# Seven-product units of the first projection, gate and up: the evacuation of a product is emitted ahead of the operands of a later one

## The chip, the cores and the metric

The kernel runs on one core of a Trainium2 chip. The metric is device time in microseconds (us); the time of a kernel is the median of several executions. Five engines matter: PE (matrix products; PEld is its weight load), ACT and DVE (elementwise work), POOL and SP (here they only issue transfers). Each engine runs its own instructions strictly in the order in which the program emits them, and waits on semaphores for what other engines or transfers have to finish first. So the place of a statement in the program is its place in the queue of its engine.

## The reference, cut to what matters

One encoder layer on 512 tokens of width 2048, in float32. The parts that the change touches are two groups of matrix products: part of the first projection, and gate and up of the feed-forward network.

```python
h = rmsnorm(x, attn_norm_w[l])
proj = h @ w_in[l]
...
aq, ak, av, gq, gk, gv, gr, glr = jnp.split(proj, split_idx, axis=-1)
...
mixed = jnp.concatenate([attn_out, gla_out], axis=-1) @ w_out[l]
x = x + mixed
h = rmsnorm(x, ffn_norm_w[l])
x = x + (jax.nn.silu(h @ w_gate[l]) * (h @ w_up[l])) @ w_down[l]
return rmsnorm(x, final_norm_w)
```

## The kernel before

**Precision.** A float32 operand is cut into a high part, rounded to the fast matrix format (`fp32r`), and a low part, the rest. A product is then high times high, high times low and low times high, added up in PSUM.

**Units.** Columns 256 at a time of a weight matrix make a unit. Its 2x2 block product is done by a scheme with seven products instead of eight (class `Units`, lines 1511 to 1654). The first projection (class `Front`, from line 1783) has 16 units: four of the output gate, four of the gated linear attention's q and k, eight of the attention's q and k. Gate and up (class `Feed`, from line 1656) have 44 units, gate and up in turn; the first two are done otherwise, and 42 go through the loop that the change touches.

**Steps.** A unit has seven steps, n = 0 to 6; step i of a stage is product n of unit u. Each product is 8 matmuls of 512 columns with the high part (line 1601) and 8 of 256 columns with the low part (line 1604). The products n = 0 to 6 go to the PSUM banks X, V, Y, X, W, Z, W, so several products add to a bank that an earlier one, or an evacuation, has filled.

**Operands** (`lead(i)`, called two steps ahead of product i): ACT casts the block to its high part (`cast`, line 1563), DVE adds two blocks for the product after that where n = 0, 1, 2 or 5 needs a sum (`add`, line 1538 and its neighbours: all four record as L1538), DVE subtracts the high part from the block to get the low part (`sub`, line 1569).

**Evacuation** (`evac_(i)`, called through `evac_late()` one step after product i was emitted). What it does depends on n:

- n = 0: ACT writes -X into bank Y (L1629)
- n = 1: ACT copies V to SBUF (L1632)
- n = 2: ACT writes -Y into bank W (L1636), DVE writes V - Y into bank Z (L1638)
- n = 3: ACT copies half of X (L1623), DVE adds the other half (L1624): one quarter of the unit's output tile, which is taken here
- n = 4: DVE adds W to the copy of V (L1645) and folds its halves into the output tile (L1647); product 6 adds to W and has to wait for L1645 to have read it
- n = 5, n = 6: a quarter of the output each (L1623, L1624); after n = 6 `finish` is queued for the next `run_urgent()`, which comes after the products of that step

`finish` scales the output tile on DVE (L1801 or L1799 in `Front`; L1727 for gate, L1734 for up) and POOL issues a store of it to DRAM, 512 KB (line 1802; line 1736 for up). Then the tile is given back.

**Tiles.** Blocks, sums, high parts, low parts and output tiles are all large tiles (`b` in the profile, 33 in the kernel). They are handed out first in, first out: `get` takes the tile that was given back longest ago, and the first instruction that writes it waits until the last user of the tile is done, be it PE, DVE or a store. `fetch()` (line 1524) is called at the head of each step: SP issues loads of weight blocks, 512 KB each, as long as fewer than 8 blocks are held and more than 3 tiles are free. A load waits on SP in the same way for the last user of its tile.

**The order of a step** is written out by hand in the two loops (lines 1766 and 1813): `fetch`, `lead` of the product two steps on, `evac_late` of the product before, then this step's products, then `run_urgent`.

Of the kernel before, what the change touches and what calls it, by code (L numbers as in the profile page):

```python
# [114 lines left out]
def put(*slots):  # L115
    for s in slots:
        if s.home is not None:
            s.home.free.append(s.i)


def layer(nc, tc, x, attn_norm_w, w_in, rel_table, gw_f, gb_f, gw_b, gb_b, gla_norm_w, w_out,
# [7 lines left out]
    with tc.manual_schedule(), \  # L129
# [136 lines left out]
        def run_urgent():  # L266
            while urgent:
                try:
                    next(urgent[0])
                    break  # L270
                except StopIteration:
                    urgent.popleft()
# [295 lines left out]
        def read_qk(pr):  # L568

            f = 1 - pr % 2  # L570
            if pr < NH // 2:
                mine = qkr[pr] = [[s2.get(F32R) for _ in range(2)] for _ in range(2)]
                for n in range(2):
                    for i in range(2):
                        src = qkd[pr // 2 * 2 + i][64 * n:64 * n + 64, f * 512:(f + 1) * 512]
                        for r in (slice(0, 64), slice(64, 128)):
                            pool.dma_start(out=mine[i][n].f[r], in_=src)
                            yield
# [168 lines left out]
        def attention():  # L747
# [7 lines left out]
            for u in range(UNITS + 5):  # L755
                h = u // 4
                if u < UNITS:
# [7 lines left out]
                    while h // 2 not in ready:  # L765
                        run_urgent()
                run(att_scores, u)
                run(att_round, u - 3)
                run(att_exp, u - 1)
                if u % 2 == 0:  # L770
                    run(att_lift, (u - 6) // 2, UNITS // 2)
# [65 lines left out]
        def gla_operands():  # L837
            G["raw"] = s2.get(F32, [P, KT, 32])
            sp.dma_start(out=G["raw"].t, in_=w_in[:, C_LR:C_LR + 32].rearrange("(k p) c -> p k c", p=P))
# [22 lines left out]
        def low_rank_weights():  # L862

            raw = G.pop("raw")
            w = G["w"] = [s2.get(F32R, [P, 8, 64]) for _ in range(2)]
            for i in range(2):
                r = raw.t[:, i * 8:(i + 1) * 8]
                act.copy(w[i].t[:, :, 0:32], r)
                dve.tensor_tensor(w[i].t[:, :, 32:64], r, w[i].f[:, :, 0:32], op=OP.subtract)
            put(raw)  # L870
# [785 lines left out]
        class Feed(Blocks, Units):  # L1656
# [82 lines left out]
            def run(self):  # L1739
                banks = {}  # L1740
                for i, (u, q) in enumerate(self.seq):
                    if u not in banks:
                        banks[u] = [ps.get() for _ in range(4)]
                    self.most = 5 if i < 2 else 3
                    self.load()
                    if i >= 5:
                        self.fetch((2, 3, 4)[i - 5])
                    self.split(i)
                    self.sums(i + 1)
                    self.sums(i + 2)  # L1750
                    self.split(i + 1)
                    if i < 2:
                        self.sums(self.n_sums, halves=True)
                    if i >= self.n - 2:
                        self.lead(i - self.n + 2)
                    self.pieces(i, banks[u])
                    done = None
                    if q == self.per - 1:
                        done = self.evac(u, banks.pop(u))
                        for _ in range((0, 2)[u]):  # L1760
                            next(done)
                    for _ in range(3 if i < 2 else 2):
                        run_urgent()
                    if done:
                        urgent.append(done)
                for i, (u, n) in enumerate(self.steps):
                    self.fetch()
                    self.lead(i + self.AHEAD)
                    self.evac_late()
                    self.products(i)  # L1770
                    if u == len(self.units) - 1:
                        if n in self.FREES:
                            for q in range(NP):
                                put(*xs[q]["slots"][self.FREES[n]])
                        if n in (1, 3, 5, 6):
                            down_start((1, 3, 5, 6).index(n))
                    for _ in range(2 if i < 7 else 1):
                        run_urgent()
                self.evac_late()
# [3 lines left out]
        class Front(Units):  # L1783
# [27 lines left out]
            def run(self):  # L1811
                assert len(xi) == NP
                for i, (u, n) in enumerate(self.steps):
                    self.fetch()
                    self.lead(i + self.AHEAD)
                    self.evac_late()
                    if u == len(self.units) - 1:
                        if n in (0, 2, 4):
                            st.until, st.limit = in_pieces, n // 2 + 1
                            st.load()  # L1820
                        if n == 6:
                            st.split(jobs[n_front].first + 2)
                    self.products(i)
                    if u == len(self.units) - 1:
                        if n in (4, 6):
                            for q in range(NP):
                                put(*xi[q]["slots"][self.FREES[n]])
                        if n == 4:
                            for _ in read_qk(0):
                                pass  # L1830
                        if n == 5:
                            gla_operands()
                    run_urgent()
                low_rank_weights()
                self.evac_late()
                run_urgent()
# [27 lines left out]
        def down_start(q):  # L1864
            if q == 0:
                g_load(0)
            if q == 1:
                st.until = down_pieces
                st.limit = 3
                st.load()  # L1870
                g_load(1)
            if q == 2:
                g_split(0)
                st.split(down_first + 2)
            if q == 3:
                dn.make(1)
# [497 lines left out]
```

## Time and profile before

| | us |
|---|---|
| time before, median of 3 runs (2161.77 to 2163.85) | 2162.83 |
| the profiled execution's own time | 2165.34 |
| its span in the trace | 2163.6 |
| PE busy | 2135.8 (99% of the span) |
| DVE busy | 1724.6 (80%) |
| ACT busy | 1229.1 (57%) |

Stages named here: `Front`, the units of the first projection, is in the stretch 105 to 450 us of the span; the loop of `Feed` is in 895 to 1720 us.

How to read the rows that follow. A row of the timeline has start and length in us, engine, line of the kernel, operation, output <- input by the program's names (a: small tiles, b: large tiles, ps: PSUM), shapes and count; in square brackets, how long the engine was idle before it, and what ended that. SPq and POOL rows with `DMA_DIRECT2D` are the issue of a transfer, not its run. A row of waits has total us, times, longest. A row of issues ends with the time from issue to landing. The row GB/s of a window gives the traffic in 40 equal slices of it. Busy PE is not PE at its peak, since matmuls are pipelined and their ends are modelled.

### The profile page before, as it was taken

How to read it: one execution, taken by the hardware profiler on the slowest of the kernel's cores; microseconds unless marked ns; L12 is line 12 of the kernel's file. 1: busy time of each engine (PE TensorE's matmuls, PEld its weight loads, DVE VectorE, ACT ScalarE, POOL GpSimd, SP SyncE). 2: the span in 40 equal slices, each digit the busy share in tenths (PEclk: the TensorE clock that was granted, in tenths of full speed). 3: DMA queues.
4: the chain of work that ended last, by engine and by line, in shares of the span. 5: the costliest groups of instructions: out<-in, count | busy, mean ns of one | idle time of the engine just before them, and what ended most of it. 6: DMA issues, size and time to landing. Idle time of an engine off the chain costs nothing.

```text
span 2163.6 us, 30507 instructions
## 1 busy us (share of the span) xinstructions
PE 2135.8 (99%) x11418; PEld 1835.3 (85%) x11418; DVE 1724.6 (80%) x2345; ACT 1229.1 (57%) x2051; POOL 172.6 (8%) x278
## 2 busy tenths in 40 slices
PE   9999999999999999999999999999999999999998
PEld 7887888888888888988888888888888888888887
DVE  5677787868877657988888888888888878897885
ACT  7444444457786545555545555555555576666762
POOL 0000000112312000000000000000000020232000
PEclk9999999999999999999999999999999999999999
DMA  6543444365754423444434334443344497899572
GB/s 203 172 149 108 136 120 134 105 199 171 201 199 140 134 98 117 137 127 123 116 113 136 116 118 117 127 132 112 114 130 117 173 241 248 200 256 241 194 256 78
DMA packets 340594, 330.47 MB, mean 153 GB/s; under 512 B 15133, under 2 KB 260365, under 8 KB 340446
## 3 DMA queue, kind: packets, MB, share of 16 engines
q1 hardware_dynamic: 313598, 258.07, 39.1%
q0 software_dynamic: 26528, 69.91, 12.5%
q8 instruction: 90, 1.47, 0.3%
q14 instruction: 58, 0.48, 0.1%
q10 hardware_dynamic: 320, 0.53, 0.1%
HBM read 267.55 MB, written 60.92 MB: 152 GB/s over the span
## 4 chain that ended last, share of the span: by engine, by line
PE 83%; issue 13%; DMA 1%; DVE 1%; ACT 1%; POOL 0%; DVEq 0%; SPq 0%; POOLq 0%; ACTq 0%
PE ps L1601 26%; PE ps L1604 14%; PE ps L349 6%; PE ps L350 6%; PE ps L348 6%; PE ps L2057 5%; PE ps L2056 5%; PE ps L2055 5%; PE ps L699 1%; PE ps L2270 1%; PE ps L2272 1%; PE ps L2271 1%; PE ps L643 1%; PE ps L724 1%; PE ps L723 1%
## 5 line engine op out<-in xcount | busy, mean ns | idle before, releaser
L1569 DVE TENSOR_TENSOR b<-b,b 128x1024 fp32r<-128x1024 f32 x406 | 495.2, 1220 | 133.9 <-ACT b L1563 122.0
L1563 ACT CAST b<-b 128x1024 fp32r<-128x1024 f32 x406 | 425.9, 1050 | 200.7 <-DVE b L1569 92.0
L1601 PE MATMUL ps<-a,b 128*128 128x512 f32 x1656 | 427.0, 393 | 16.4 <-DVE a L1645 11.1
L1601 PE MATMUL ps<-b,b 128*128 128x512 f32 x1592 | 421.2, 393 | 0.5 <-ACT ps L1629 0.5
L1601 PEld LDWEIGHTS ps<-a,b 128*128 128x128 f32 x1656 | 304.8, 189 | 81.9 <-issue 13.2
L1601 PEld LDWEIGHTS ps<-b,b 128*128 128x128 f32 x1592 | 280.2, 189 | 43.2 <-ACT ps L1629 0.7
L1538 DVE TENSOR_TENSOR b<-b,b 128x1024 f32<-128x1024 f32 x232 | 282.6, 1218 | 1.3 <-PE ps L350 0.7
L1604 PEld LDWEIGHTS ps<-b,b 128*128 128x128 f32 x1592 | 232.6, 190 | 23.4
L1604 PE MATMUL ps<-a,b 128*128 128x256 f32 x1656 | 242.9, 283 | 0.0
L1604 PE MATMUL ps<-b,b 128*128 128x256 f32 x1592 | 242.8, 282 | 0.0
L1604 PEld LDWEIGHTS ps<-a,b 128*128 128x128 f32 x1656 | 225.2, 192 | 8.5
L1623 ACT COPY b<-ps 128x256 f32<-128x256 f32 x174 | 64.6, 371 | 223.5 <-PE ps L1604 223.5
L2031 DVE TENSOR_TENSOR b<-b,b 128x1024 fp32r<-128x1024 f32 x112 | 136.5, 1220 | 34.8 <-ACT b L2023 34.8
L348 PE MATMUL ps<-b,b 128*128 128x512 f32 x344 | 139.8, 407 | 0.0
L350 PE MATMUL ps<-b,b 128*128 128x512 f32 x344 | 135.1, 393 | 0.0
L349 PE MATMUL ps<-b,b 128*128 128x512 f32 x344 | 134.9, 392 | 0.0
L2023 ACT CAST b<-b 128x1024 fp32r<-128x1024 f32 x112 | 116.6, 1052 | 26.6 <-DVE b L2011 15.3
L220 DVE TENSOR_TENSOR b<-b,b 128x512 fp32r<-128x512 f32 x120 | 79.5, 683 | 26.7 <-ACT b L239 26.5
L1624 DVE TENSOR_TENSOR b<-b,ps 128x256 f32<-128x256 f32 x174 | 72.2, 415 | 27.7 <-ACT b L1623 27.7
L2055 PE MATMUL ps<-b,a 128*128 128x512 f32 x240 | 93.4, 389 | 0.0
L2056 PE MATMUL ps<-b,a 128*128 128x512 f32 x240 | 93.4, 389 | 0.0
L2057 PE MATMUL ps<-b,a 128*128 128x512 f32 x240 | 93.4, 389 | 0.0
(308 smaller groups left out, 3580.6 us busy)
## 6 DMA issues: line engine op xcount, KB each, us to landing
b<-in_w_in_dram SPq DMA_DIRECT2D x94, 512.0 KB, 4.1
b<-in_w_gate_dram SPq DMA_DIRECT2D x88, 512.0 KB, 4.4
b<-in_w_up_dram SPq DMA_DIRECT2D x88, 512.0 KB, 3.8
b<-in_w_down_dram SPq DMA_DIRECT2D x88, 512.0 KB, 6.9
b<-in_w_out_dram SPq DMA_DIRECT2D x32, 512.0 KB, 4.4
md<-a POOLq DMA_DIRECT2D x56, 256.0 KB, 6.8
gd<-b POOLq DMA_DIRECT2D x22, 512.0 KB, 5.3
b<-gd SPq DMA_DIRECT2D x22, 512.0 KB, 5.5
```

The costliest lines, as they stand in the source:

```text
L348: mm(o, xh.t[:, c], wh.t[:, w], start=first and not on, stop=False, skip_group_check=on)
L349: mm(o, xh.t[:, c], wl.t[:, w], start=False, stop=False, skip_group_check=on)
L350: mm(o, xl.t[:, c], wh.t[:, w], start=False, stop=last, skip_group_check=on)
L1538: tt = lambda o, x_, y_: dve.tensor_tensor(o.t, x_.t, y_.t, op=OP.add)
L1563: act.copy(hi.t, home[key].t)
L1569: dve.tensor_tensor(lo.t, home[key].t, hi.f, op=OP.subtract)
L1601: mm(o.rearrange("p (s t) -> p s t", s=2), hi.t[:, q], self.xs[q][self.ORDER[n]], start=new and q == 0, stop=False, skip_group_check=True)
L1604: mm(o[:, 0:256], lo.t[:, q], self.xs[q][self.ORDER[n]][:, 0], start=False, stop=q == NP - 1, skip_group_check=True)
L2031: dve.tensor_tensor(lo.t, s.t, hi.f, op=OP.subtract)
L2055: mm(o, xh[:, t], wh, start=new and j == 0, stop=False, skip_group_check=True)
L2056: mm(o, xh[:, t], wl, start=False, stop=False, skip_group_check=True)
L2057: mm(o, xl[:, t], wh, start=False, stop=last and j == 1, skip_group_check=True)
```

## The change

In both loops `evac_late()` moves from behind `lead(i + AHEAD)` to ahead of it. Nothing is added or taken away.

```diff
                 for i, (u, n) in enumerate(self.steps):
                     self.fetch()
+                    self.evac_late()
                     self.lead(i + self.AHEAD)
-                    self.evac_late()
                     self.products(i)
                     if u == len(self.units) - 1:
                         if n in self.FREES:
...
                 for i, (u, n) in enumerate(self.steps):
                     self.fetch()
+                    self.evac_late()
                     self.lead(i + self.AHEAD)
-                    self.evac_late()
                     if u == len(self.units) - 1:
                         if n in (0, 2, 4):
                             st.until, st.limit = in_pieces, n // 2 + 1
```

On ACT the cast of product i + 2 now stands behind the evacuation of product i - 1, and on DVE the sum and the subtraction do. The output tile of a unit (taken by the evacuation of n = 3) is taken ahead of that step's high, sum and low tiles instead of behind them.

## The prediction

> **What bounds the kernel now.** I read first the windows of the two stages that the change touches, then who PE waited for in each (first two waits: 105 to 450 us; third: 895 to 1720 us).
>
> ```profile
> 105.00:450.00 345.00, 328.62 (x1839) 284.74 (x1838) 267.00 (x294) 157.77 (x219) 14.75 (x28) 1.00 0.46 133
> 895.00:1720.00 825.00, 824.54 (x4726) 725.55 (x4725) 700.72 (x760) 429.14 (x594) 11.17 (x21) 1.00 0.42 123
> ...
> PE ps L1601 <- DVE a L1645: 11.1, 12, 1.1
> PE ps L1601 <- ACT ps L1629: 3.5, 1, 3.5
> ...
> PE ps L1601 <- ACT ps L1629: 0.5, 1, 0.5
> ```
>
> `Feed` is bound by PE: 824.54 of 825 us busy, one wait of 0.5 us. There is nothing else to win there. In `Front` PE idles 16.4 us (345.00 - 328.62). Twelve units lose about 0.9 us each because product 6 waits for L1645, and 3.5 us go at the start. So I read one unit of `Front` in the timeline, from one scaling of an output tile to the next.
>
> ```profile
> 239.04 1.23 DVE L1801 TENSOR_TENSOR b<-b,a 128x1024 f32<-128x1024 f32 x1
> ...
> 240.56 0.53 POOL L1802 DMA_DIRECT2D gfd<-b  x1 [20.09 <-DVE b L1801]
> ...
> 243.53 1.05 ACT L1563 CAST b<-b 128x1024 fp32r<-128x1024 f32 x1 [3.33 <-DMA gfd<-b]
> ...
> 244.61 1.22 DVE L1569 TENSOR_TENSOR b<-b,b 128x1024 fp32r<-128x1024 f32 x1 [2.07 <-ACT b L1563]
> ...
> 246.95 1.23 DVE L1569 TENSOR_TENSOR b<-b,b 128x1024 fp32r<-128x1024 f32 x1 [1.12 <-ACT b L1563]
> ...
> 248.10 0.69 DVE L1638 TENSOR_TENSOR ps<-a,ps 128x512 f32<-128x512 f32 x1
> ...
> 248.69 1.22 DVE L1538 TENSOR_TENSOR b<-b,b 128x1024 f32<-128x1024 f32 x1
> ...
> 250.97 0.41 DVE L1624 TENSOR_TENSOR b<-b,ps 128x256 f32<-128x256 f32 x1
> ...
> 251.30 1.22 DVE L1538 TENSOR_TENSOR b<-b,b 128x1024 f32<-128x1024 f32 x1
> ...
> 253.57 0.68 DVE L1645 TENSOR_TENSOR a<-a,ps 128x512 f32<-128x512 f32 x1
> ...
> 254.39 2.08 PE L1601 MATMUL ps<-a,b 128*128 128x512 f32 x8 [0.85 <-DVE a L1645]
> ...
> 254.62 1.22 DVE L1538 TENSOR_TENSOR b<-b,b 128x1024 f32<-128x1024 f32 x1
> ...
> 255.76 1.22 DVE L1569 TENSOR_TENSOR b<-b,b 128x1024 fp32r<-128x1024 f32 x1
> ...
> 258.09 1.22 DVE L1569 TENSOR_TENSOR b<-b,b 128x1024 fp32r<-128x1024 f32 x1 [0.78 <-ACT b L1563]
> ...
> 259.23 0.41 DVE L1624 TENSOR_TENSOR b<-b,ps 128x256 f32<-128x256 f32 x1
> ...
> 259.68 1.22 DVE L1799 SCALAR_TENSOR_TENSOR b<-b,a 128x1024 f32<-128x1024 f32 x1
> ...
> 260.06 1.78 PE L1601 MATMUL ps<-a,b 128*128 128x512 f32 x7
> ...
> 262.85 2.00 PE L1601 MATMUL ps<-a,b 128*128 128x512 f32 x8
> ...
> 263.04 1.00 SPq L1531 DMA_DIRECT2D b<-in_w_in_dram  x2
> ```
>
> This is a **loop through a store**. The output tile is scaled (239.04) and stored (240.56). The cast of product 4 is handed that very tile and waits until the store has landed (243.53, idle 3.33 for the store). Subtraction 4, cast 5, subtraction 5 follow, and DVE works on without a pause until it waits for one cast (258.09) and scales the next tile (259.68). The loop takes 259.68 - 239.04 = 20.64 us. PE needs 2.79 us a product (262.85 - 260.06), 19.5 us a unit. PE waits out the difference at L1645.
>
> **The change part by part.** Per step ACT's evacuation moves ahead of one cast, DVE's ahead of at most one sum and one subtraction. Neither helper issues a transfer, so SP's and POOL's queues keep their order; PE's too, since only the evacuation holds matmuls there.
>
> *The loop, DVE's part.* Three terms change.
> - L1638 moves ahead of subtraction 5, into DVE's wait for cast 5 (idle 1.12 at 246.95): 248.69 - 248.10 = 0.59 off.
> - The last L1624 moves ahead of subtraction 2, into the 0.78 idle at 258.09: 259.68 - 259.23 = 0.45 off.
> - The L1624 of n = 5 loses that cover and stands ahead of a sum: 0.33 on (251.30 - 250.97).
>
> Those of n = 3 and n = 4 stay inside the loop. Sum: 20.64 - 0.59 - 0.45 + 0.33 = **19.93 us**, still over PE's 19.5.
>
> *The loop, the store's part.* L1645 gets ahead of a sum and a subtraction, while the scaling stays behind all of them. From L1645 to the scaling it is 6.11 us now (259.68 - 253.57). Then it is: 1.05 to the next sum (254.62 - 253.57), sum 1.14 (255.76 - 254.62), subtraction 1.14, L1624 0.33, sum 1.14, 2.33 between the last two subtractions (258.09 - 255.76), subtraction 1.14; together 8.27. PE runs on from L1645: product 2 of the next unit starts 262.85 - 253.57 = 9.28 behind it. That frees product 1's low tile, and SP issues two weight loads 0.19 later (263.04). The store is issued 1.52 behind the scaling (240.56 - 239.04). The first load follows the scaling by 3.36 now (263.04 - 259.68), and by 9.28 + 0.19 - 8.27 = 1.20 then. So **the load goes from 1.84 us behind the store to 0.32 ahead of it.** The second load needs a tile that a sum frees, 1.14 + 1.14 + 1.22 = 3.5 behind the scaling.
>
> What such a meeting costs shows in `Feed`: its up units issue the same store (landing us: `Front`'s median in the first row, min, median, max of `Feed`'s 22 in the second), a load 0.27 ahead of it (939.82, 940.09).
>
> ```profile
> gfd<-b POOLq DMA_DIRECT2D x4, 512.0 KB, 2.9
> ...
> DMA to landing us min/median/max: 2.9/5.3/6.3
> ...
> 939.82 6.74 SPq L1531 DMA_DIRECT2D b<-in_w_gate_dram  x3
> 940.09 0.54 POOL L1736 DMA_DIRECT2D gd<-b  x1 [35.26 <-DVE b L1734]
> ...
> GB/s 0 0 0 0 0 0 0 0 0 0 0 20 59 193 225 219 207 197 242 217 361 408 432 432 426 328 180 49 0 0 0 0 0 0 43 113 152 272 319 342
> ```
>
> The last row is the traffic from 938 to 948 us, 0.25 us a slice: about 2.5 us at some 220 GB/s, then 1.5 at 430. The store seems to wait out the load. In `Feed` nobody needs its tile at once; in `Front` a cast does. Call d what the landing takes beyond 2.9. Bounds: 0 (no meeting; less than 0 is excluded, since 2.9 is `Feed`'s minimum too) and 6.3 - 2.9 = 3.4. I take the nearest row, the median: **d = 5.3 - 2.9 = 2.4**, and a loop of 19.93 + 2.4 = 22.33 us, 1.7 more than now. Nothing corrects it: scaling and load both hang on L1645. Of the second load I count nothing; it is what the upper bound is for.
>
> *Start and end.* Here the trace reads:
>
> ```profile
> 114.18 1.04 ACT L1563 CAST b<-b 128x1024 fp32r<-128x1024 f32 x1 [2.42 <-DMA vd<-b]
> 115.13 0.58 ACT L1629 ACTIVATE ps<-ps 128x512 f32<-128x512 f32 x1
> ...
> 117.54 1.22 DVE L1569 TENSOR_TENSOR b<-b,b 128x1024 fp32r<-128x1024 f32 x1
> ...
> 133.38 1.22 DVE L1801 TENSOR_TENSOR b<-b,a 128x1024 f32<-128x1024 f32 x1
> ...
> 383.80 1.23 DVE L1801 TENSOR_TENSOR b<-b,a 128x1024 f32<-128x1024 f32 x1
> ...
> 399.89 2.06 PE L1601 MATMUL ps<-a,b 128*128 128x512 f32 x8 [1.06 <-DVE a L1645]
> ```
>
> The 3.5 us wait goes: L1629 no longer queues behind the cast at 114.18. PE doesn't keep it, because DVE is next: from subtraction 4 (117.54), DVE's chain needs the loop without its store, 19.93 - (244.61 - 239.04) = 14.36, so the first scaling comes at 131.90 (now 133.38). The last stalled product is that of 399.89, product 6 of the fourteenth unit; its scaling before is that of 383.80, the thirteenth, twelve loops behind the first. Afterwards no blocks are left to load, tiles are plenty, and PE sets the pace. From a scaling to that product it takes 19.93 - 8.27 + (254.39 - 253.57) = 12.48, plus d. After: 131.90 + 12 x 22.33 + 12.48 + 2.4 = 414.74, that is 14.85 later than 399.89. In general the change is 13 d - 16.35, and it breaks even near d = 1.3.
>
> *Feed.* Its loop hides the store (no wait on it), so the order costs DVE cover only. DVE works 700.72 us in 42 units, 16.7 of 19.6 each; the tightest result, L1645, comes ahead of a sum and a subtraction instead of behind them. I count no loss. The start's 0.5 goes, since L1629 no longer stands behind a cast. If the cover is gone after all, each 0.1 us a unit costs 42 x 0.1 = 4.2.
>
> *Sum.* +14.85 - 0.5 = +14.4 us. The profiled execution took 2165.34, 2.5 above the median of the runs; on it 2179.7, on the median 2162.83 + 14.4 = **2177.2 us**.
>
> **A rule weighed.** The traffic row says that the store waits while the load runs. The Trainium skill, "DMA: Bandwidth & Descriptors", section "Queues, rings and completion order", says that each DMA engine takes turns between its queues, packet by packet. By that the two would share; the row's 220 followed by 430 GB/s speaks for the waiting, so I keep the row's price. What sharing would give is the second rival.
>
> **The rivals.**
> 1. *The store stays clear of the load* (d near 0), so the shorter loop pays. For it: `Front`'s stores land in 2.9 today, and my 0.32 is a difference of chains of seven terms; half a microsecond of DVE less would turn the order round. Against it: at equal issue the two still meet. Time: -16.35 - 0.5 = -16.8; with the strays of today's loop, (383.80 - 133.38) - 12 x 20.64 = 2.7 and (399.89 - 383.80) - (254.39 - 239.04) = 0.7, it is -13.4: **2149.4**. This is the other side: one mechanism, the landing, decides at d = 1.3.
> 2. *Store and load take turns.* The store alone bursts 1.4 us (524 KB at the 430 GB/s of the late slices is 1.2); turns would at most double that: d = 1.4, 13 x 1.4 - 16.8 = +1.4, **2164.2**. Against it: the median of 5.3.
> 3. *The second load is waited out too.* d = 3.4, 13 x 3.4 - 16.8 = +27.4, **2190.2**. For it: the load is issued 2 us behind the store, while the store is still waiting. Against it: by then the store's packets are queued.
>
> That the order doesn't change is no case: the program fixes it.
>
> **How the numbers follow.** Forecast (d about 2 to 3) 0.50, rival 3 and beyond 0.17, rival 2 0.11, rival 1 0.22. A measurement here tells 0.2% (4.3 us) from no change: slower means d above 1.6, faster d below 1.0. So slower 0.67, same 0.11, faster 0.22. Cases of both signs hold the range: from rival 1, 2149, to just past rival 3, 2191. The forecast's own range, d from 2 to 3, is 2172 to 2185.
>
> **What would show it.** Right: in `Front` the store's landing near 5.3, the cast's wait for it longer than 3.33, scalings 22.3 apart, PE waiting for the cast or L1636 at product 4 and for L1645 at product 6, no 3.5 us at the start; `Feed` as before, with its 0.5 gone. Wrong: scalings 19.9 apart with landings of 2.9 (rival 1), near 21.3 (2) or beyond 23 (3); any PE wait that recurs in `Feed`; or a tile that a cast is handed with another last user than today, which would break the loop I summed.

## The result, and the profile after

| | median us | runs |
|---|---|---|
| before | 2162.3 | 2160.89 to 2163.85, 4 |
| after | 2176.94 | 2171.53 to 2178.09, 4 |

The ratio is 1.0063, with a 95% interval of 1.0044 to 1.0082: slower by 14.6 us, where 2177.2 us was forecast. The profiled execution took 2178.09 us (forecast 2179.7), its span is 2176.3.

The windows of the two stages (`Front`, then the loop of `Feed`) in the changed kernel:

```profile
105.00:450.00 345.00, 318.65 (x1759) 276.65 (x1758) 256.90 (x280) 153.38 (x206) 13.48 (x26) 0.98 0.43 119
...
905.00:1735.00 830.00, 830.00 (x4765) 730.88 (x4765) 710.12 (x769) 427.25 (x599) 11.17 (x21) 1.00 0.42 124
```

`Feed` now has no gap at all. `Front`'s stretch holds 80 matmuls fewer than before (1759 against 1839): there the time went. Who PE waited for in it:

```profile
PE ps L1601 <- ACT ps L1636: 21.8, 10, 3.5
PE ps L1601 <- DVE a L1645: 4.5, 9, 0.6
```

Before, L1645 had 11.1 us and the start 3.5. That part of the change worked: the start's wait is gone, and L1645 comes earlier. A new wait takes their place, product 4 for L1636, which on ACT stands behind the cast that waits for the store. One unit in the timeline of the changed kernel, from scaling to scaling:

```profile
242.53 1.22 DVE L1801 TENSOR_TENSOR b<-b,a 128x1024 f32<-128x1024 f32 x1
...
243.72 2.74 SPq L1531 DMA_DIRECT2D b<-in_w_in_dram  x2
...
244.04 0.53 POOL L1802 DMA_DIRECT2D gfd<-b  x1 [23.57 <-DVE b L1801]
...
249.76 1.04 ACT L1563 CAST b<-b 128x1024 fp32r<-128x1024 f32 x1 [5.45 <-DMA gfd<-b]
...
250.71 0.58 ACT L1636 ACTIVATE ps<-ps 128x512 f32<-128x512 f32 x1
...
250.84 1.22 DVE L1569 TENSOR_TENSOR b<-b,b 128x1024 fp32r<-128x1024 f32 x1 [4.82 <-ACT b L1563]
...
251.34 1.88 PE L1601 MATMUL ps<-a,b 128*128 128x512 f32 x7 [2.08 <-ACT ps L1636]
...
251.98 0.69 DVE L1638 TENSOR_TENSOR ps<-a,ps 128x512 f32<-128x512 f32 x1
...
253.18 1.23 DVE L1569 TENSOR_TENSOR b<-b,b 128x1024 fp32r<-128x1024 f32 x1 [0.51 <-ACT b L1563]
...
256.92 0.68 DVE L1645 TENSOR_TENSOR a<-a,ps 128x512 f32<-128x512 f32 x1
...
257.75 2.06 PE L1601 MATMUL ps<-a,b 128*128 128x512 f32 x8 [0.55 <-DVE a L1645]
...
265.19 1.22 DVE L1799 SCALAR_TENSOR_TENSOR b<-b,a 128x1024 f32<-128x1024 f32 x1
```

Read it from the top. The load is issued at 243.72, the store at 244.04: 0.32 us ahead, to the hundredth as summed. The cast waits 5.45 us for the store (3.33 before), L1636 follows it at 250.71, and PE has stood for 2.08 us. L1638 now lies in DVE's wait for cast 5. From L1645 to the next scaling it is 8.27 us (265.19 - 256.92), the sum of the prediction. The whole loop takes 22.66.

Whose packets moved is in the rows of the two queues (packets, MB, share), first from 245 to 247 us, then from 247 to 249; q1 carries the loads, q0 the store:

```profile
q1 hardware_dynamic: 615, 0.31, 80.7%
...
q0 software_dynamic: 139, 0.52, 63.5%
q1 hardware_dynamic: 536, 0.27, 44.4%
```

The store was issued at 244.04; alone, its bytes move from 1.0 to 2.4 us after the issue. Here, with the loads on the way, q0 has not a single packet up to 247, 3 us after the issue, and then all its 0.52 MB go in 2 us. The same two rows for the 4 us behind the issue, 244.04 to 248.04, say how much went first:

```profile
q1 hardware_dynamic: 1040, 0.52, 58.9%
q0 software_dynamic: 57, 0.23, 14.2%
```

The 1040 packets and 0.52 MB of q1 are one load, the one ahead; the second load, issued behind the store, is not yet among them. The store waits until the load ahead of it has gone; the two do not take turns. Whether it is held in its queue or on the way from POOL's issue into the queue, no row here shows.

### The profile page after: what moved, and what is told of

The parts are those of the page before. It is cut to its first block, busy times and chain, and to the rows that moved or that the text cites. A ratio compares the mean times of both kernels' runs of the same rounds, so it can differ in the third digit from the quotient of the medians.

```text
span 2176.3 us, 30564 instructions
## 1 busy us (share of the span) xinstructions
PE 2139.1 (98%) x11418; PEld 1837.9 (84%) x11418; DVE 1727.0 (79%) x2345; ACT 1226.5 (56%) x2051; POOL 172.5 (8%) x278
## 3 DMA queue, kind: packets, MB, share of 16 engines
q0 software_dynamic: 26528, 69.91, 12.5%
## 4 chain that ended last, share of the span: by engine, by line
PE 83%; issue 13%; DMA 1%; DVE 1%; POOL 0%; ACT 0%; SPq 0%; DVEq 0%; POOLq 0%; ACTq 0%
PE ps L1601 26%; PE ps L1604 14%; PE ps L350 6%; PE ps L349 6%; PE ps L348 6%; PE ps L2057 5%; PE ps L2055 5%; PE ps L2056 4%; PE ps L699 1%; PE ps L643 1%; PE ps L723 1%; PE ps L724 1%; PE ps L2272 1%; PE ps L2270 1%; PE ps L2271 1%
```

## The experiments

The quoted texts say what was expected of each run before it was made.

**e1 and e2: each loop alone.** The edit of the change in `Front` alone, then in `Feed` alone.

> The new order in Front alone, the old one in Feed. My theory (the whole loss is Front's loop through the store): 2162.3 + 14.9 = 2177 us, units of Front 22.5 us apart, stores landing in about 5.5 us; only Feed's 0.5 us wait at its start comes back. Rival A (the order costs DVE cover in Feed's 42 units, and that is what was lost): near 2162 or below, with Front's shorter DVE chain even 2149. Rival B (half and half): about 2170.

> The new order in Feed alone. My theory: 2161.8 us, the 0.5 us wait at Feed's start gone and nothing else; no PE wait in Feed. Rival A: up to 15 us slower, 2177. Rival B: about 2169.

Measured: `Front` alone 2177.66 us against 2162.31, ratio 1.0071 (1.0056 to 1.0086). `Feed` alone 2162.09, ratio 0.9996 (0.9987 to 1.0006). All of the loss is `Front`'s; in `Feed` the order makes no difference that can be measured. Rivals A and B fall.

**e3 and e4: the loads held until the store has landed.**

```diff
                     self.evac_late()
                     self.lead(i + self.AHEAD)
+                    if n == 2:
+                        sp.dma_start(out=held[u], in_=self.both[i + 2][0].f[0:1, 0])
```

e3 does this in the new order, e4 in the old one. The small transfer reads the high tile of product 4, so SP stands there until the cast that waits for the store is done; the loads are queued behind it.

> Both loops in the new order, and in each unit of Front SP issues a 512-byte transfer out of the high tile of product 4 before the next two weight loads, so that these cannot be issued before the cast that waits for the store is done. Order of ACT and DVE and the tiles handed out are those of the change. My theory (the store waits for the load that is ahead of it): stores land in 2.9 us, units 19.9 us apart, 13 x 0 - 16.8 us on 2162.3: 2145.5. Rival (the casts are late because evacuations stand ahead of them, and the landing is only what is seen of it): units still 22 us apart, about 2177. Rival (turns: the store loses 1.4 us to any load): about 2164.

> The old order with the same held loads: the control for e3. My theory: each unit 20.64 us, the strays of landings over 2.9 us (3.5 us in all) gone: 2159. If holding the loads costs something by itself (a load that comes too late, a busy SP): above 2162.3, and e3 has to be read against it. If the loads had no part in the strays: 2162.

Measured: e3 2148.96 us, ratio 0.9937 (0.992 to 0.9953): 13.3 us faster than the kernel before, 28 faster than the change. One unit of e3 in the timeline:

```profile
251.87 1.22 DVE L1801 SCALAR_TENSOR_TENSOR b<-b,a 128x1024 f32<-128x1024 f32 x1
...
253.38 0.53 POOL L1804 DMA_DIRECT2D gfd<-b  x1 [19.40 <-DVE b L1801]
...
256.35 1.05 ACT L1563 CAST b<-b 128x1024 fp32r<-128x1024 f32 x1 [2.69 <-DMA gfd<-b]
...
257.43 0.25 SPq L1820 DMA_DIRECT2D held<-b  x1
...
257.78 10.00 SPq L1531 DMA_DIRECT2D b<-in_w_in_dram  x4
...
271.80 1.22 DVE L1803 TENSOR_TENSOR b<-b,a 128x1024 f32<-128x1024 f32 x1
```

The loads come behind the cast, and the loop takes 271.80 - 251.87 = 19.93 us, the prediction's sum with nothing added for a later landing. ACT and DVE run in the order of the change; only the meeting of load and store is gone. So it is the meeting that costs, and the order by itself gains. The run is 3.5 us above the 2145.5 expected; two late landings, 4.1 and 4.0 us instead of 2.9, are 2.3 of that.

e4, the control, is 2163.2 us, ratio 1.0003 (0.9994 to 1.0012). Holding the loads costs nothing that can be measured, but my 2159 was a miss: the late landings of the old order are still there, with the loads far away. For the one issued at 195.05 us in e4, the queues and the landing in the 4 us behind the issue:

```profile
q0 software_dynamic: 142, 0.52, 33.5%
q8 instruction: 1, 0.02, 1.5%
...
grd<-b POOLq DMA_DIRECT2D x1, 512.0 KB, 4.7
```

A packet of the instruction queue q8 is there. In e3 and e4 each store of `Front` that landed later than 3.2 us had one in the 4 us behind its issue (e3: 4.1 and 4.0; e4: 4.7 and 3.5), and no other one of the loop's stores had one of q8. That is a coincidence, not an experiment, and e5 and e6 weaken it: seven of their stores had such a packet, and four of these landed in 2.9 to 3.2.

**e5 and e6: the store's tile out of the loop.** `Front` holds at most 6 blocks instead of 8, so its queue of free tiles is two longer, and the tile of the store goes to a weight load.

```diff
+            def fetch(self, most=6):
+                Units.fetch(self, most)
+
             def place(self, u):
                 return self.units[u]
```

> The old order; Front holds at most 6 blocks instead of 8, so two more tiles are free and the tile of the store is handed to a weight load (which nobody waits for soon) instead of to the cast of product 4. My theory (the loop through the store bounds Front): no loop, PE sets the pace after the 3.5 us wait at the start, product 6 of the fourteenth unit at about 383.3 us instead of 399.9: 2162.3 - 16.6 = 2145.7 us. Rival (DVE is too busy for PE's pace, whatever tile a cast gets): units stay near 20.6 us, 2160 to 2163. Rival (6 blocks are too few, loads come late): slower, with casts waiting for loads.

> The new order with at most 6 blocks. My theory: the same, and without the 3.5 us wait at the start and its slow clock: product 6 of the fourteenth unit at about 378.5 us: 2162.3 - 21.4 - 0.5 = 2140.4 us; landings may still be 5 us, without a wait for them. Rival (the loss comes from the order of casts behind evacuations): slower than e5 by the 14.6 us of the change, about 2160.

Measured: the old order (e5) 2142.37 us, ratio 0.9907 (0.9892 to 0.9922); the new order (e6) **2140.81 us**, ratio 0.9898 (0.9884 to 0.9913). Both beat both kernels. `Front`'s window in e5:

```profile
105.00:450.00 345.00, 344.70 (x1945) 299.60 (x1944) 282.33 (x325) 170.91 (x247) 20.89 (x40) 1.00 0.51 147
```

PE is busy for 344.70 of 345 us, and scalings are 19.55 us apart. What waits for the 14 stores issued up to 400 us in e5 is now SP with its loads, up to 12.5 us each. DVE was never too slow for PE: in either order the loop through the store was what kept `Front` behind PE's pace. e5 came 3.3 us below its 2145.7, because the 3.5 us wait at the start, which I had left in, is not in it either. Without the loop the change costs nothing: the old order keeps a 0.5 us wait at the start of `Feed`, which the new one has not; the medians are 1.6 apart, each compared with the kernel before rather than with each other.

**e7: at most 7 blocks, new order.** The edit of e6 with 7.

> The new order with at most 7 blocks: one more free tile, so the store's tile goes to the low tile of product 4 (the subtraction waits for the store, not the cast: 1.08 us less in the loop), the cast of product 5 no longer waits for subtraction 4 (1.2 us less), and both loads of the step are issued ahead of the store. My theory (the store waits out every load issued ahead of it, 2.4 us each): landing 2.9 + 4.8 = 7.7 us, loop 19.93 - 2.28 + 4.8 = 22.5 us, about as slow as the change, 2177. If it waits out one load only: landing 5.3, loop 20.1 us, about 2148.

Measured: 2166.4 us, ratio 1.0018 (1.0009 to 1.0028), between the two values. The timeline of one unit of e7, and then the row of the landing of its store (us from issue):

```profile
260.21 0.53 POOL L1805 DMA_DIRECT2D gfd<-b  x1 [21.65 <-DVE b L1802]
...
267.09 1.23 DVE L1569 TENSOR_TENSOR b<-b,b 128x1024 fp32r<-128x1024 f32 x1 [4.90 <-DMA gfd<-b]
...
268.23 0.69 DVE L1638 TENSOR_TENSOR ps<-a,ps 128x512 f32<-128x512 f32 x1
...
268.83 1.22 DVE L1569 TENSOR_TENSOR b<-b,b 128x1024 fp32r<-128x1024 f32 x1
```

```profile
gfd<-b POOLq DMA_DIRECT2D x1, 512.0 KB, 6.8
```

The subtraction waits for the store, as said. Two loads ahead, issued 1.25 and 0.29 us before this store, make the landing 6.8, 3.9 more than alone: neither one load's 2.4 nor twice that. In the 4 us behind its issue q1 moved 1846 packets and the store 6, so part of the second load went ahead of it too. (The thirteen stores of the loop land in 5.0 to 7.2.) And L1638 is back in the loop (268.83 - 268.23 = 0.60), since cast 5 no longer makes DVE wait. With that the loop should be 19.93 - 2.28 + 0.6 + 3.9 = 22.15; from the scaling at 258.70 to that at 280.83 it is 22.13.

**e8: only the second of the two loads held, new order.**

```diff
+                    if n == 3:
+                        self.fetch(min(8, len(self.quads) + 1))
+                        sp.dma_start(out=held[u], in_=self.both[i + 1][0].f[0:1, 0])
                     self.fetch()
```

> The new order; of the two weight loads of step 3 in Front the first is issued as in the changed kernel, the second held (as in e3) until the cast that waits for the store is done. My theory (the first load, 0.32 us ahead of the store, is what it waits out; the second costs nothing): landings 5.3 to 5.5 us, units 22.3 us apart, 2175 to 2177 us, as the change. Rival (the second load, issued 2 us behind the store, is what delays it): landings near 2.9 to 4, 2149 to 2163. If both have a share: between, near 2170.

Measured: 2173.72 us, ratio 1.0049 (1.0032 to 1.0066), a little under the forecast. SP in the timeline of one unit of e8 and the landing of its store (issued at 264.17):

```profile
263.84 0.37 SPq L1531 DMA_DIRECT2D b<-in_w_in_dram  x1
...
270.79 0.25 SPq L1818 DMA_DIRECT2D held<-b  x1
...
271.13 0.37 SPq L1531 DMA_DIRECT2D b<-in_w_in_dram  x1
```

```profile
gfd<-b POOLq DMA_DIRECT2D x1, 512.0 KB, 5.5
```

With the second load out of the way the store still lands at 5.5. The first load, 0.33 us ahead, is what it waits out. In five of e8's loops the load came 0.4 us behind the store instead, and those stores landed in 3.6 to 3.7 us; that fits a time a little under the forecast.

## Why the prediction was right

*The bound.* `Front` was held by the loop through the store, and `Feed` by PE: shown by e1, e2 and by e5, where one number takes the tile out of the loop and PE waits 0.2 us in all.

*The loop's DVE part, 19.93 us.* Shown by e3, to the hundredth.

*The order of load and store.* 0.32 us ahead, as summed. That the meeting is what costs is shown by e3 against the change: 28 us apart with the same order on ACT and DVE.

*The landing.* Summed with 5.3; most stores of the changed kernel land in 5.4 to 5.7. The store waits the load out; the turns by packet that the Trainium skill states ("DMA: Bandwidth & Descriptors", "Queues, rings and completion order") are not seen in the rows of the queues here: one whole load, 1040 packets, went first.

*The new wait.* Product 4 for L1636 and product 6 for L1645, as named.

*The sum.* The fourteenth unit's product 6 was summed to 414.74 and started at 413.96. Four sizes behind that were off, and they nearly offset each other:

- The first scaling came at 129.78, not 131.90. The stage before had been 2.1 us faster in that execution, and it is no part of the change: e4, in the old order, shows 1.9 of it. Counted from the first product of `Front` (106.31 before, 104.19 after) the first scaling came 1.48 us sooner, as summed.
- "Nothing corrects it" was wrong. In three of the twelve loops the store landed in 3.9 us, and the loop took 20.9. The rows below are from the changed kernel: PE clock by windows, then the timeline.

```profile
160.00:164.00 4.00, 3.08 (x11) 2.57 (x12) 3.08 (x4) 2.19 (x4) 0.00 (x0) 0.77 0.03 8
164.00:168.00 4.00, 4.00 (x22) 3.60 (x21) 3.96 (x6) 2.11 (x2) 0.00 (x0) 0.80 0.34 86
```

```profile
160.92 2.29 PE L1601 MATMUL ps<-a,b 128*128 128x512 f32 x7 [1.93 <-ACT ps L1636]
...
165.15 2.23 PE L1601 MATMUL ps<-b,b 128*128 128x512 f32 x8
...
176.28 0.53 POOL L1802 DMA_DIRECT2D grd<-b  x1 [22.00 <-DVE b L1801]
...
176.74 0.37 SPq L1531 DMA_DIRECT2D b<-in_w_in_dram  x1
```

  Behind a wait the granted clock fell to 0.77, and product 4 took 165.15 - 160.92 = 4.23 us instead of 2.79. That used up PE's wait for L1645 and more: product 6 of that unit started 15.92 us behind the scaling, instead of 15.22 in the unit shown above. So the next load, which follows PE, was issued at 176.74, 0.46 behind the store instead of 0.32 ahead. The store kept its place, and the next unit came sooner. The same pair, a slow product 4 and then a landing of 3.9, recurs from 273.85 and from 362.48.
- The other nine loops took more than 22.33: 22.5 to 22.7, and one 24.1. That one's store landed in 7.1 us, with a packet of the instruction queue behind its issue.
- From the thirteenth scaling to the fourteenth unit's product 6 it took 413.96 - 397.27 = 16.69 us, against the 14.88 summed. The store in it landed in 6.3 us instead of 5.3, and behind the wait of 2.71 us that followed, the granted clock fell to 0.58 (408 to 412 us).

The mean of the twelve loops is (397.27 - 129.78) / 12 = 22.29 us, against the 22.33 of the prediction. Counted from the first product, the whole stretch grew by 16.2 us, against the 14.85 summed. That the forecast of 2177.2 fits the median of 2176.94 this closely is in part luck: the four runs alone lie between 2171.53 and 2178.09. The sign and the mechanism are not luck.

*The rivals.* The one on the other side, a store clear of the load, was priced at 2149.4; e3 makes it true and takes 2148.96. Turns, priced at 2164.2, would have made landings of 2.9 + 1.4 = 4.3 us; most are 5.4 to 5.7. The wait for the second load, priced at 2190.2, is excluded by e8.

## What to carry to other kernels

Where a tile goes straight from a store to the next user, the landing is part of a loop, and its length hangs on which transfers are issued just ahead; look up from both sides what an edit does to that order, even if it moves no transfer. Here the new order shortened DVE's part of the loop by 0.71 us and lost more than that, because the load, which follows PE, moved 2.16 us forward against the store. The cheaper cure here was one number, the depth of the prefetch: two free tiles more took the store out of the loop and were worth more than either order.

## What the runs showed of the hardware

- A 512 KB store issued 0.3 us behind a 512 KB load moved no packet for 3 us and mostly landed in 5.4 to 5.7 us instead of 2.9; issued 0.4 to 0.5 us ahead of it, in 3.6 to 3.9; with two loads ahead, in 5.0 to 7.2. The transfer that came first moved its data first, though the two come from different queues.
- A packet of the instruction queue behind a store's issue went with a later landing: 4.8 and 3.6 us in the kernel before, 4.7 and 3.5 in e4, and in the changed kernel 5.0 for the store at 422.10, when no weight block was left to load. It isn't the whole of it: the store of the kernel before at 176.20 landed in 3.5 with no such packet behind it, and in e5 and e6, where seven stores had one, three landed in 3.9 to 4.1 (packet about 0.5 us behind the issue) and four in 2.9 to 3.2 (packet 2.4 to 3.4 us behind it). The cause stays open.
- PE's granted clock fell after some waits and not after others: in the changed kernel to 0.77 after 1.93 us and not at all after 3.52 us, in the kernel before to 0.57 after 3.51 us. What decides it stays open.
